# Modulation rows of parts two to five moved beside the output projections, and read as whole rows

## The chip, the cores and the metric

The kernel runs on one core of one Trainium2 chip. The metric is the device time of one execution in microseconds, the median of several runs. Engines are named as in the profile: PE is TensorE (PEld its weight loads), DVE is VectorE, ACT is ScalarE, POOL is GpSimd, SP is SyncE, which issues most transfers.

## The reference, cut to what matters

One decoder layer on a sequence of 512 tokens of width 1024, all in float32. Six modulation vectors of 1024 values each come from the condition vector, and are needed at very different times:

```
mod = (silu(c) @ w_ada + b_ada)          # w_ada is 1024 x 6144
sh1, sc1, g1, sh2, sc2, g2 = split(mod, 6)
h = rms(x) * (1 + sc1) + sh1
x = x + g1 * mixer(h)                    # SSD, attention and pooling, then w_out
h = rms(x) * (1 + sc2) + sh2
x = x + g2 * (relu(h @ w_ff1)**2 @ w_ff2)
```

Parts zero and one (sh1, sc1) are needed at once. Part two (g1) is needed after w_out, parts three and four (sh2, sc2) in the second norm, part five (g2) in the second feed-forward product. The mixer projects h by w_in to the inputs of three branches and three gates, and adds

```
sigmoid(gate_ssd) * (y_ssd @ w_ssd_out) + sigmoid(gate_attn) * (y_attn @ w_attn_out) + sigmoid(gate_pool) * (y_pool @ w_pool_out)
```

## The kernel before

Activations lie transposed, 128 channels by 512 tokens a block. Every float32 operand of a large product is split into a high and a low part (h and l in the names); a product is three matmuls, low by high, high by high and high by low (`mm3`, L293 to L296). Weights come in pairs of 128 rows: `wstream` (L283) loads a pair (`raw`, four buffers, 0.5 MB, L287), ACT rounds it to the high part `wh` (L279), DVE subtracts to the low part `wl` (L280); `wh` and `wl` have three buffers each. One pair feeds 24 matmuls in `gemm_feat` (L298) or `gemm_tok` (L310). After each pair `wstream` calls `tick` (L263).

`tick` is where other work is traced between the matmuls. It runs one piece of the list `side`, which holds the steps of attention, SSD and pooling, and on every second call one piece of the list `background`. That list has 32 pieces, `ada_later(part, k)` for parts two to five and eight values of k. One piece makes 128 values of one modulation vector, with `ada_load` (L237) and `ada_dot` (L243): 128 rows of the transposed w_ada, 1024 values each, are loaded as two halves of 128x512 into two blocks; each half is multiplied on DVE with `crow`, the silu of the condition copied to all partitions, and summed along the row (L246); the two sums are added (L248) and the bias added (L256) into a column of `modv`.

The order of the products after the first two (Q0 and K0, ordered by hand in a manual schedule up to about 60 us) is, in the names used below: Q1, K1, Q2, K2, V0, V1, V2 (attention inputs), BCC, XS0, Z0, XS1, Z1 (SSD inputs), gate GA0, attention projection, GA1, attention projection, U0, U1 (pool inputs), gate GS0, SSD projection, GS1, SSD projection, GP0, pool projection, GP1, pool projection, then w_out and the feed-forward part. Each has four pairs of weights and so four ticks, the two attention projections two. Before the change the 32 pieces therefore fall on the 64 ticks of Q1 to U0.

The SSD heads (`ssd_heads`, L904) broadcast rows of a small table `prow` to all partitions with a transfer each (`M`, L912), DVE and ACT make decay factors from it (L917 to L926), and PE uses them (L932); `ssd_states` makes the tiles X (L882) and prev (L895) from which PE makes the states. `project` (L747) multiplies a branch's product with its gate `sg` on DVE (L751).

Blocks of 128x512 come from a ring of 49 places (`blk`, `free`): the place that was given back first is taken first, and a new tile in a place waits until all users of the old one are done. Beside it there are four places of twice that size with the names L0, L1, N0 and N1 (pool `exp`): they hold the tokens in another order for Q1 to V2, then the attention output `oh`, `ol` until the second attention projection, and from w_out on two pairs of the first feed-forward weights (L1130), later sums of weights.

Outside the manual schedules a planner orders each engine's instructions by their place in the trace, with `high_priority` stretches moved ahead and with work that is ready taken forward into idle time, and it sets the semaphores. Each engine then runs its list in order. So does SP: a transfer that waits for its place holds all transfers behind it on SP's queue.

Of the kernel before, what the change touches and what calls it, by code (L numbers as in the profile page):

```python
# [10 lines left out]
F32 = mybir.dt.float32  # L11
F32R = mybir.dt.float32r
AF = mybir.ActivationFunctionType
ALU = mybir.AluOpType
# [3 lines left out]
P = 128  # L18
D = 1024
T = 512  # L20
# [78 lines left out]
def kernel(ctx: ExitStack, tc: tile.TileContext, a: dict, out: bass.AP, dbg=None):  # L99
    nc = tc.nc  # L100
# [5 lines left out]
    exp = ctx.enter_context(tc.tile_pool(name="exp", bufs=1))  # L106
# [6 lines left out]
    def uid(s):  # L113
        cnt[0] += 1
        return f"{s}_{cnt[0]}"

    class Slots:
# [12 lines left out]
        def free(self, t):  # L130
            self.idle.append(self.used.pop(id(t))[0])
# [3 lines left out]
    def blk(name, dt=F32):  # L135
        return sb.take(name, dt)
# [12 lines left out]
    def small(shape, name, bufs=1, dt=F32):  # L149
        return sm.tile(shape, dt, tag=name, name=uid(name), bufs=bufs)  # L150
# [7 lines left out]
    def show(name, ap):  # L158
        if dbg is not None:
            dbg(name, ap)  # L160

    mm = nc.tensor.matmul
    V, S = nc.vector, nc.scalar
# [20 lines left out]
    crow2 = small([P, 2, T], "crow")  # L184
    crow = [crow2[:, i, :] for i in range(2)]
# [3 lines left out]
    def vc(name, i=0, n=1):  # L189
        return vec[:, VCOLS[name][0] + i : VCOLS[name][0] + i + n]  # L190
# [43 lines left out]
        return sums  # L234


    def ada_load(part, k):  # L237
        wa = [blk("wa") for _ in range(2)]
        for i in range(2):
            nc.sync.dma_start(wa[i], a["w_ada"][part * 8 + k][:, i * T : (i + 1) * T])  # L240
        return wa

    def ada_dot(wa, o):  # L243
        d = small([P, 2], "dot", 4)
        for i in range(2):
            V.scalar_tensor_tensor(wa[i], wa[i], 1.0, crow[i], ALU.mult, ALU.mult, accum_out=d[:, i : i + 1])  # L246
        free(*wa)
        V.tensor_tensor(o, d[:, 0:1], d[:, 1:2], ALU.add)  # L248

    modv = small([P, 4, 8], "modv")  # L250

    def ada_later(part, k):
        def go():
            o = modv[:, part - 2, k : k + 1]
            ada_dot(ada_load(part, k), o)
            V.tensor_tensor(o, o, vc("b_ada", part * 8 + k), ALU.add)  # L256
        return go


    background = [ada_later(part, k) for part in (2, 3, 4, 5) for k in range(8)]  # L260
    side, ticks = [], [0]

    def tick(n=1):  # L263
        ticks[0] += 1
        for _ in range(n):
            if side:
                side.pop(0)()
        if ticks[0] % 2 == 0 and background:
            background.pop(0)()

    def flush():
        while side:
            side.pop(0)()
# [9 lines left out]
    def wstream(w, nk, ch, k0=0, ahead=None):  # L283
        for kp in range(nk // 2):
            with tc.high_priority(offset=AHEAD if ahead is None else ahead):
                raw = raws.tile([P, 2, T], F32, tag="raw", name=uid("raw"))
                nc.sync.dma_start(raw, w[ch, k0 // 2 + kp])  # L287
                wh, wl = wsplit(raw, [P, 2, T])
            for i in range(2):
                yield 2 * kp + i, wh[:, i, :], wl[:, i, :]  # L290
            tick()
# [6 lines left out]
    def gemm_feat(w, nk, ch, ah, al, k0=0):  # L298

        ps = [acc() for _ in range(4)]  # L300
        for k, wh, wl in wstream(w, nk, ch, k0):
            for j in range(4):
                cs = slice(j * P, (j + 1) * P)
                mm3(ps[j], wh[:, cs], wl[:, cs], ah[k], al[k], k == 0, k == nk - 1)
        return ps
# [13 lines left out]
    def split(x, name):  # L319
        h, l = blk(name + "h", F32R), blk(name + "l", F32R)  # L320
        S.copy(h, x)
        V.tensor_tensor(l, x, h.bitcast(F32), ALU.subtract)
        return h, l
# [17 lines left out]
    with tc.manual_schedule(engines={E.DVE, E.Activation, E.PE, E.SP}):  # L341
# [14 lines left out]
        def ada_whole(part, k):  # L356
            pool, tag = homes["rrrhlhlrrrhlhlhl"[2 * k + 1 - part]]
            w = pool.tile([P, 2, T], F32, tag=tag, name=uid("wada"))
            src = a["w_ada"][part * 8 + k].rearrange("p (i t) -> p i t", i=2)
            if k:  # L360
                nc.sync.dma_start(w, src)
            else:
                for i in range(2):
                    nc.sync.dma_start(w[:, i, :], src[:, i, :])
            return w
# [5 lines left out]
        wa = [ada_whole(1, 0), ada_whole(0, 0)]  # L371
# [77 lines left out]
        var, rt, r, t = (small([P, 4], "rx" + n) for n in "vryt")  # L449
# [59 lines left out]
        for k in range(8):  # L509
# [8 lines left out]
            if k < 7:  # L518
                wa = [ada_whole(1, k + 1), ada_whole(0, k + 1)]
                w_load(k + 1)  # L520
                d = small([P, 2], "dot", 4)
# [221 lines left out]
    def gate(c, ch):  # L743
        ps = gemm_feat(w_in, 8, c + ch, hh, hl)
        return evac(ps, "sg", AF.Sigmoid)

    def project(w, nk, ch, yh, yl, sg, first=False, last=False):  # L747
        ps = gemm_feat(w, nk, ch, yh, yl)
        with tc.high_priority(offset=SOON):
            for j in range(4):  # L750
                V.tensor_tensor(sg[j], ps[j], sg[j], ALU.mult)  # L751
        free(*ps)
        for j in range(4):
            if first:
                mixed.append(sg[j])
                continue
            m = mixed[4 * ch + j]
            V.tensor_tensor(m, m, sg[j], ALU.add)
            free(sg[j])
            if last:  # L760
                x, y = split(m, "mx")
                free(m)
                mh.append(x)
                ml.append(y)
        if ch == 1:
            free(*yh, *yl)


    v3 = lambda t: t.rearrange("p (c h) -> p c h", h=16)
    st = {}  # L770

    def ssd_steps():

# [329 lines left out]
    for ch in range(2):  # L1103
        sg = gate(GS, ch)
        flush()
        project(a["w_ssd_out"], 8, ch, yh, yl, sg)
    show("yn", [h.bitcast(F32) for h in yh + yl])
    show("pool", [h.bitcast(F32) for h in ph_ + pl_])
    for ch in range(2):
# [374 lines left out]
```

## Time and profile before

| | before |
|---|---|
| median of 3 runs | 1096.73 us (1096.44 to 1097.73) |
| the profiled execution | 1098.25 us |
| its span, first to last instruction | 1096.5 us |
| granted TensorE clock | 1.000 |
| PE busy | 1087.1 us, 99% of the span |
| DVE busy | 717.4 us, 65% |
| ACT busy | 527.8 us, 48% |
| products with `crow` of parts two to five | 64, 43.1 us, mean 688 ns |
| idle time of DVE before them | 20.0 us |
| half rows loaded | 64 of 256 KB, median 3.6 us to landing |

A row of a group has the line, the engine, the operation, what it writes and reads, the shapes and the count, then busy time, the mean of one, and the idle time of the engine just before with what ended it. A row in order of time has the start, the duration and the count; in square brackets stands the idle time before it and what ended that. A row of a line or tile has the shortest, median and longest duration in ns and the first and last start in us. A row of waits says who waited for whom, the sum in us, how often, and the longest.

### The profile page before, as it was taken

What the parts mean: (1) busy time and instruction counts of PE and PEld (TensorE: products, weight loads), DVE (VectorE), ACT (ScalarE), POOL (GpSimd) and SP (SyncE); (2) the same over time, 40 slices, a digit from 0 to 9 for tenths busy, and PEclk for the clock granted to TensorE, in tenths of its full rate; (3) what the DMA queues carried; (4) which work ended last, traced back from release to release, by engine and by line L of the source; (5) the groups of instructions that cost most, each with busy time, mean ns of one, the idle gap of its engine ahead of it and who ended that gap; (6) DMA issues with size and microseconds to landing.
All of it is one profiled execution on the core that took longest, in us unless ns stands there. A gap on an engine that the chain in (4) does not pass through costs nothing.

```text
span 1096.5 us, 14976 instructions
## 1 busy us (share of the span) xinstructions
PE 1087.1 (99%) x5806; PEld 927.0 (85%) x5806; DVE 717.4 (65%) x1383; ACT 527.8 (48%) x845; POOL 3.6 (0%) x10
## 2 busy tenths in 40 slices
PE   9999999999999999999999999999999999999998
PEld 7878888888887877888888888899889989989987
DVE  8975874582776778568843424577787587686664
ACT  8965875543695536625432123354344334335330
POOL 0000000000000000000000000000000000000000
PEclk9999999999999999999999999999999999999999
DMA  9853342443542354321232325360214224134032
GB/s 349 306 183 98 128 134 86 152 168 102 173 125 87 117 181 136 104 97 58 96 115 97 106 96 163 97 230 1 79 57 154 65 90 136 59 114 135 20 116 77
DMA packets 46666, 133.98 MB, mean 122 GB/s; under 512 B 5362, under 2 KB 6130, under 8 KB 46596
## 3 DMA queue, kind: packets, MB, share of 16 engines
q1 hardware_dynamic: 45392, 130.28, 36.0%
q0 software_dynamic: 480, 1.57, 0.5%
q10 hardware_dynamic: 724, 1.18, 0.3%
q8 instruction: 45, 0.74, 0.3%
q14 instruction: 25, 0.20, 0.1%
HBM read 130.89 MB, written 2.13 MB: 121 GB/s over the span
## 4 chain that ended last, share of the span: by engine, by line
PE 87%; ACT 4%; DVE 3%; DMA 3%; issue 1%; SPq 0%; ACTq 0%; DVEq 0%
PE psacc L294 22%; PE psacc L296 22%; PE psacc L295 22%; PE psacc L1345 11%; PE psacc L534 4%; DMA M<-prow 2%; PE psS L613 1%; DMA wa<-in_w_ada_dram 1%; DVE conv L850 1%; ACT wh L279 1%; PE pso L729 1%; PE pso L727 1%; DVE wl L280 1%; PE pskT L597 0%; PE psqT L592 0%
## 5 line engine op out<-in xcount | busy, mean ns | idle before, releaser
L280 DVE TENSOR_TENSOR wl<-raw,wh 128x1024 fp32r<-128x1024 f32 x140 | 171.0, 1222 | 192.2 <-ACT wh L279 190.9
L279 ACT CAST wh<-raw 128x1024 fp32r<-128x1024 f32 x140 | 146.8, 1050 | 241.1 <-PE psacc L295 168.8
L294 PE MATMUL psacc<-hl,wh 128*128 128x512 f32 x416 | 166.6, 401 | 3.4 <-DVE X L882 2.2
L295 PE MATMUL psacc<-hh,wh 128*128 128x512 f32 x416 | 162.1, 390 | 0.0
L296 PE MATMUL psacc<-hh,wl 128*128 128x512 f32 x416 | 162.0, 390 | 0.0
L295 PE MATMUL psacc<-ah,wh 128*128 128x512 f32 (+1 forms) x260 | 100.4, 386 | 0.0
L294 PE MATMUL psacc<-al,wh 128*128 128x512 f32 (+1 forms) x260 | 100.4, 386 | 0.0
L296 PE MATMUL psacc<-ah,wl 128*128 128x512 f32 (+1 forms) x260 | 100.3, 386 | 0.0
L294 PEld LDWEIGHTS psacc<-hl,wh 128*128 128x128 f32 x416 | 78.2, 188 | 21.7 <-DVE X L882 2.7
L295 PEld LDWEIGHTS psacc<-hh,wh 128*128 128x128 f32 x416 | 78.2, 188 | 16.9 <-issue 1.4
L296 PEld LDWEIGHTS psacc<-hh,wl 128*128 128x128 f32 x416 | 78.1, 188 | 16.7
L294 PE MATMUL psacc<-wl,rh 128*128 128x512 f32 x192 | 76.9, 401 | 0.0
L296 PE MATMUL psacc<-wh,rl 128*128 128x512 f32 x192 | 75.5, 393 | 0.0
L295 PE MATMUL psacc<-wh,rh 128*128 128x512 f32 x192 | 75.3, 392 | 0.0
L296 PEld LDWEIGHTS psacc<-ah,wl 128*128 128x128 f32 x260 | 48.8, 188 | 9.9
L294 PEld LDWEIGHTS psacc<-al,wh 128*128 128x128 f32 x260 | 48.9, 188 | 9.7
L295 PEld LDWEIGHTS psacc<-ah,wh 128*128 128x128 f32 x260 | 48.9, 188 | 9.6
L1405 DVE SCALAR_TENSOR_TENSOR xr<-psacc,modv,xr 128x512 f32<-128x512 f32 (+1 forms) x65 | 44.7, 739 | 18.6 <-PE psacc L296 18.6
L246 DVE SCALAR_TENSOR_TENSOR wa<-wa,crow 128x512 f32<-128x512 f32 x64 | 43.1, 688 | 20.0 <-DMA wa<-in_w_ada_dram 20.0
L296 PEld LDWEIGHTS psacc<-wh,rl 128*128 128x128 f32 x192 | 36.0, 188 | 7.6
L294 PEld LDWEIGHTS psacc<-wl,rh 128*128 128x128 f32 x192 | 36.1, 188 | 7.3 <-ACT qT L593 0.2
L295 PEld LDWEIGHTS psacc<-wh,rh 128*128 128x128 f32 x192 | 36.1, 188 | 7.0
(408 smaller groups left out, 2360.8 us busy)
## 6 DMA issues: line engine op xcount, KB each, us to landing
raw<-in_w_in_dram SPq DMA_DIRECT2D x80, 512.0 KB, 3.5
raw<-in_w_ff_dram SPq DMA_DIRECT2D x52, 512.0 KB, 3.7
wa<-in_w_ada_dram SPq DMA_DIRECT2D x64, 256.0 KB, 3.6
wada<-in_w_ada_dram SPq DMA_DIRECT2D x14, 512.0 KB, 7.8
rawl<-in_w_ff_dram SPq DMA_DIRECT2D x12, 512.0 KB, 3.5
wst<-in_w_in_dram SPq DMA_DIRECT2D x16, 256.0 KB, 7.8
M<-prow SPq DMA_DIRECT2D x16, 256.0 KB, 3.8
raw<-in_w_ssd_out_dram SPq DMA_DIRECT2D x8, 512.0 KB, 3.5
```

What stands on the lines that cost most here:

```text
L246: V.scalar_tensor_tensor(wa[i], wa[i], 1.0, crow[i], ALU.mult, ALU.mult, accum_out=d[:, i : i + 1])
L279: S.copy(wh, raw)
L280: V.tensor_tensor(wl, raw, wh.bitcast(F32), ALU.subtract)
L294: mm(ps, lhsT=wh, rhs=xl, start=first, stop=False)
L295: mm(ps, lhsT=wh, rhs=xh, start=False, stop=False)
L296: mm(ps, lhsT=wl, rhs=xh, start=False, stop=last)
L534: mm(ps[j], lhsT=t[:, j, :], rhs=w, start=first, stop=last)
L613: mm(so[b], lhsT=qT[:, b * P : (b + 1) * P], rhs=kT[:, (b + 1) * P - n : (b + 1) * P], start=True, stop=True)
L727: mm(od, lhsT=vs[kb][:, hs], rhs=pT[b // 2][:, cs : cs + P], start=(b == 0), stop=False, skip_group_check=True)
L729: mm(ov[:, b, :], lhsT=vs[b][:, hs], rhs=pT[0][:, b * P : (b + 1) * P], start=False, stop=(gi == 2 and b == 3), skip_group_check=True)
L1345: mm(o, lhsT=x[:, cs], rhs=y, start=first and k == 0 and j == 0 and n == 0, stop=k == 3 and n == 2, skip_group_check=True)
L1405: V.scalar_tensor_tensor(xT[d][:, ts], p[:, : ts.stop - ts.start], modv[:, 3, d : d + 1], xT[d][:, ts], ALU.mult, ALU.add)
```

## The change

Three things change together. A piece of `background` loads one whole row of 128x1024 with one transfer of 0.5 MB into one of the four wide places (L0, L1, N0, N1 in turn), multiplies and sums it with one DVE instruction straight into `modv`, and adds the bias; the halves, their two blocks of the ring and the add of two sums are gone. `tick` runs as many pieces as `st["pace"]` says: none up to and in the first SSD gate GS0, two in each of the two SSD projections, one in the products behind the first of them (GS1, GP0, the first pool projection and GP1). With four ticks each these are 8, 4, 8, 4, 4 and 4 pieces. And the dictionary `st` is made earlier in the text, since `tick` reads it.

```
-    def ada_load(part, k):
-        wa = [blk("wa") for _ in range(2)]
-        for i in range(2):
-            nc.sync.dma_start(wa[i], a["w_ada"][part * 8 + k][:, i * T : (i + 1) * T])
-        return wa
-
-    def ada_dot(wa, o):
-        d = small([P, 2], "dot", 4)
-        for i in range(2):
-            V.scalar_tensor_tensor(wa[i], wa[i], 1.0, crow[i], ALU.mult, ALU.mult, accum_out=d[:, i : i + 1])
-        free(*wa)
-        V.tensor_tensor(o, d[:, 0:1], d[:, 1:2], ALU.add)
-
     modv = small([P, 4, 8], "modv")
 
     def ada_later(part, k):
         def go():
             o = modv[:, part - 2, k : k + 1]
-            ada_dot(ada_load(part, k), o)
+            w = exp.tile([P, 2, T], F32, tag=("L0", "L1", "N0", "N1")[k % 4], name=uid("wada"))
+            nc.sync.dma_start(w, a["w_ada"][part * 8 + k].rearrange("p (i t) -> p i t", i=2))
+            V.scalar_tensor_tensor(w, w, 1.0, crow2, ALU.mult, ALU.mult, accum_out=o)
             V.tensor_tensor(o, o, vc("b_ada", part * 8 + k), ALU.add)
         return go
...
-    side, ticks = [], [0]
-
-    def tick(n=1):
-        ticks[0] += 1
-        for _ in range(n):
-            if side:
-                side.pop(0)()
-        if ticks[0] % 2 == 0 and background:
-            background.pop(0)()
+    side, st = [], {}
+
+    def tick():
+        if side:
+            side.pop(0)()
+        for f in background[: st.get("pace", 0)]:
+            f()
+        del background[: st.get("pace", 0)]
...
     for ch in range(2):
         sg = gate(GS, ch)
         flush()
+        st["pace"] = 2
         project(a["w_ssd_out"], 8, ch, yh, yl, sg)
+        st["pace"] = 1
```

More of the change, by code (lines that the diff above doesn't have):

```diff
@@ L769 @@
     v3 = lambda t: t.rearrange("p (c h) -> p c h", h=16)
-    st = {}
     def ssd_steps():
```

## Prediction

> **What bounds the kernel now.** I read the page first, then the stretches, then what TensorE (PE) waited for, then the order of time around its two dearest waits.
>
> ```profile
> span 1096.5 us, 14976 instructions
> PE 1087.1 (99%) x5806; PEld 927.0 (85%) x5806; DVE 717.4 (65%) x1383; ACT 527.8 (48%) x845; POOL 3.6 (0%) x10
> ```
>
> PE is busy for 1087.1 of 1096.5 us. Only 9.4 us of idle time are left, and a change that takes no matmul away can win only what PE waits. By stretch (us, then PE, PEld, DVE, ACT and POOL busy, clock, DMA share, GB/s):
>
> ```profile
> 0.00:50.00 50.00, 47.63 (x233) 39.46 (x234) 44.80 (x93) 44.25 (x65) 0.20 (x4) 1.00 0.97 358
> ...
> 250.00:500.00 250.00, 246.47 (x1282) 202.19 (x1281) 163.09 (x310) 138.28 (x205) 0.00 (x0) 1.00 0.38 122
> 500.00:704.00 204.00, 204.00 (x908) 168.93 (x907) 96.32 (x149) 65.67 (x85) 0.00 (x0) 1.00 0.33 107
> ```
>
> PE idles 3.5 us between 250 and 500, in the SSD and attention part, and not at all between 500 and 704, where the branch projections run. VectorE (DVE) is 65% busy in the first of these (163.09 of 250) and 47% in the second (96.32 of 204). From 250 to 500 it also does 28 half modulation rows, and stands 12.1 us for their loads (busy, mean ns, then idle time before them):
>
> ```profile
> L246 DVE SCALAR_TENSOR_TENSOR wa<-wa,crow 128x512 f32<-128x512 f32 x28 | 19.1, 688 | 12.1 <-DMA wa<-in_w_ada_dram 12.1
> ```
>
> What ended PE's waits from 60 to 500 us (total, times, longest):
>
> ```profile
> PE psacc L294 <- DVE X L882: 2.2, 1, 2.2
> PE psacc L294 <- DVE conv L935: 0.5, 1, 0.5
> PE psacc L294 <- ACT prev L895: 0.5, 1, 0.5
> PE psacc L294 <- ACT pT L711: 0.2, 1, 0.2
> ```
>
> These are 3.4 of the 3.5 us. What one costs is read from matmul starts, since ends are modelled:
>
> ```profile
> 428.16 0.39 PE L295 MATMUL psacc<-hh,wh 128*128 128x512 f32 x1
> 428.39 0.40 PE L296 MATMUL psacc<-hh,wl 128*128 128x512 f32 x1
> 431.01 0.50 PE L294 MATMUL psacc<-hl,wh 128*128 128x512 f32 x1 [2.22 <-DVE X L882]
> 431.35 0.40 PE L295 MATMUL psacc<-hh,wh 128*128 128x512 f32 x1
> ```
> ```profile
> 387.99 0.40 PE L296 MATMUL psacc<-hh,wl 128*128 128x512 f32 x1
> 388.90 0.50 PE L294 MATMUL psacc<-hl,wh 128*128 128x512 f32 x1 [0.51 <-DVE conv L935]
> 389.23 0.40 PE L295 MATMUL psacc<-hh,wh 128*128 128x512 f32 x1
> ```
>
> Undisturbed, a matmul starts 0.23 us after the last (428.16 to 428.39). The first wait costs 2.62 - 0.23 = 2.39 before the late start and 0.34 - 0.23 = 0.11 after it: 2.50 us. The second costs 0.68 + 0.10 = 0.78. So a wait costs its idle time and 0.28 more; the 0.5 of prev is 0.78 and the 0.2 of pT 0.48. All four together are 4.5 us, **the most that can be won here**.
>
> [...]
>
> Both larger waits lead back to the modulation rows that are to be moved. On DVE in order of time:
>
> ```profile
> 385.43 0.69 DVE L246 SCALAR_TENSOR_TENSOR wa<-wa,crow 128x512 f32<-128x512 f32 x1 [1.22 <-DMA wa<-in_w_ada_dram]
> ...
> 386.96 1.23 DVE L280 TENSOR_TENSOR wl<-raw,wh 128x1024 fp32r<-128x1024 f32 x1
> 388.10 0.74 DVE L935 SCALAR_TENSOR_TENSOR conv<-conv,dcol,psy 128x512 f32<-128x512 f32 x1
> ...
> 427.29 0.68 DVE L924 TENSOR_SCALAR M<-M,pc 128x128 f32<-128x128 f32 x3 [2.92 <-DMA M<-prow]
> 427.88 2.48 DVE L751 TENSOR_TENSOR sg<-psacc,sg 128x512 f32<-128x512 f32 x4
> 430.27 0.68 DVE L882 TENSOR_TENSOR X<-psX,dt 128x512 f32<-128x512 f32 x1
> ```
>
> At 385 DVE stands 1.22 us for a row of w_ada, multiplies it, and the split of the weights and L935, for which PE waits, come behind: without the row L935 is done 2.7 us sooner (1.22, and 386.96 - 385.43 = 1.53). At 427 DVE stands 2.92 us for a broadcast of prow, and X comes behind that and the four products with sg. The chain of waits leads there from a load of w_ada (start, us):
>
> ```profile
> 396.30 4.94 DMA wa<-in_w_ada_dram
> ...
> 402.66 4.31 DMA M<-prow
> ```
>
> and on SyncE's queue the broadcasts (L912) wait for places which w_ada held before:
>
> ```profile
> SPq L912 <- DVE wa L246: 8.1, 4, 3.9
> ```
>
> **The change, part by part.** It removes 64 half-row loads, 64 products with sum and 32 adds of two halves, and moves the rest from the stages Q1 to U0 to ssd_out (two rows a tick), the second SSD gate and the two pool gates and first pool projection (one a tick): 8 + 4 + 8 + 4 + 4 + 4 = 32. Old costs:
>
> ```profile
> L240 SPq DMA_DIRECT2D wa<-in_w_ada_dram x64: 327/328/2078, 42.4 to 475.9; - x64
> L246 DVE SCALAR_TENSOR_TENSOR wa<-wa,crow x64: 679/688/696, 53.9 to 480.6; 128x512 f32<-128x512 f32 x64
> L246 DVE DVE_READ_ACCUMULATOR wa<-wa,crow x64: 78/83/93, 54.6 to 481.2; 128x1 f32 x64
> ```
> ```profile
> L248 DVE TENSOR_TENSOR modv<-dot x32: 149/157/161, 58.4 to 481.4; 128x1 f32<-128x1 f32 x32
> L256 DVE TENSOR_TENSOR modv<-modv,vec x32: 147/156/163, 58.6 to 483.7; 128x1 f32<-128x1 f32 x32
> ...
> L1116 DVE SCALAR_TENSOR_TENSOR A<-modv,vec x1: 168/168/168, 333.5 to 333.5; 128x8 f32<-128x8 f32 x1
> ```
> ```profile
> DVE wa L246 <- DMA wa<-in_w_ada_dram: 20.0, 14, 4.1
> ```
>
> From DVE before 484 us go 64 x (0.688 + 0.083) + 32 x (0.157 + 0.156) = 59.4 us of work and 20.0 us of standing for loads; SyncE's queue loses 64 issues of 0.33 and their waits ahead of weights and broadcasts. DVE has idle time there in any case, so these 79 us are worth what they held up on PE: 2.50 + 0.78 = 3.28. The other two waits were ended by ACT, and I leave them.
>
> New costs have a model in the whole rows of parts 0 and 1 at the start:
>
> ```profile
> L388 DVE SCALAR_TENSOR_TENSOR wada<-wada,crow x7: 1219/1220/1222, 19.8 to 49.8; 128x1024 f32<-128x1024 f32 x7
> ...
> DMA to landing us min/median/max: 4.4/7.8/9.0
> ```
>
> A row costs DVE 1.22 + 0.08 (reading the sum, as above) + 0.16 (bias) = 1.46 us, 46.7 us in all, and SyncE 32 issues of 0.33 us. Two rows a tick meet these stretches (first and third gemm of the SSD projection's four):
>
> ```profile
> 551.00:573.00 22.00, 22.00 (x98) 18.21 (x98) 8.71 (x11) 5.26 (x6) 0.00 (x0) 1.00 0.39 129
> ...
> 595.00:617.00 22.00, 22.00 (x98) 18.20 (x97) 6.74 (x7) 4.99 (x7) 0.00 (x0) 1.00 0.30 97
> ```
>
> Eight rows add 11.7 us: 20.4 and 18.4 busy of 22, cost nothing on PE. The cover is the split weights: three pairs of buffers hold 24 matmuls each, 5.5 us; a pair is refilled when PE has left it, so two pairs, 11.0 us, stand between DVE and PE, less cast and split, 2.5 us if the cast is no longer than the 1.23 of the split: 8.5 us. DVE has time to spare there now (waits from 551 to 704):
>
> ```profile
> DVE wl L280 <- ACT wh L279: 92.4, 24, 4.2
> ```
>
> If that cover is gone, each us that DVE is late is a us on PE. A row that has not landed holds the split behind it on DVE, and PE waits for the split; on SyncE a row whose place is not free holds the next weight load. Landing is bounded by
>
> ```profile
> raw<-in_w_ssd_out_dram SPq DMA_DIRECT2D x8, 512.0 KB, 3.5
> ```
>
> and the 7.8 us of the rows at the start, where DMA ran at 358 GB/s. Two rows and one weight load of 0.52 MB in 5.5 us ask 286 GB/s, nearer the full start, so I take 6 us. A place then turns round in 1.46 + 0.33 + 6 = 7.8 us, at 7.8 us landing in 9.6, both under the 11.0 us in which four places are asked for once.
>
> The results are read late enough: A2 (L1116), which ran at 333.5, moves behind part four, but its readers stand in the second norm after w_out; the residual of part two likewise:
>
> ```profile
> L1143 DVE SCALAR_TENSOR_TENSOR xr<-psacc,modv,xr x4: 744/744/747, 724.5 to 726.4; 128x512 f32<-128x512 f32 x4
> ```
>
> A2's early run also shows that the planner moves ready work forward, so rows may run before their ticks, in DVE's gaps.
>
> What no row shows is the new order that the planner makes of everything from 60 us on, with other blocks (64 fewer turns of the ring of 49). Bounds: all four waits gone, -4.5 us; none gone and one as dear as the dearest seen in addition, +2.5. I take the two named waits as gone and one new wait of the smallest size, 0.48: **3.28 - 0.48 = 2.8 us**. The profiled execution took 1098.25 us, 1.75 around its span; it becomes 1095.45. The median of the runs, 1096.73, lies 1.52 below it: **1093.9 us**.
>
> **The rivals.**
> *The wait at 431 stays.* What DVE stood for there is a broadcast, not a row; DMA, cast and the four products with sg are still ahead of X. For it: 2.48 us of sg lie ahead of X whatever lands. Against it: X need be only 2.22 us sooner, and the queue's 8.1 us go. Only 0.78 is won: 1096.0.
> *All four go,* because ACT's chain hangs on the same broadcasts: 1096.73 - 4.5 = 1092.2. Against it: ACT's own work is the same.
> *Slower: DVE's queue in the two projections of ssd_out.* Its idle time there falls to 1.6 and 3.6 us. With the cover of 8.5 a row may be late by (1.6 + 8.5) / 8 = 1.3 us on average before PE stands; from there each us counts eight times. Shown is 20.0 / 64 = 0.31 on average, at most 4.1. Halfway, 2.2, PE would lose 17.6 - 10.1 = 7.5 and 17.6 - 12.1 = 5.5: 1093.9 + 13 = 1106.9. Against it: the average shown, and that planned work runs ahead of its ticks.
> [...]
> *The new order has a new wait* of 2.50 and keeps the old ones: 1099.2.
>
> **How the numbers follow.** Forecast 0.44 (own range 1092.9 to 1094.8), the wait stays 0.32, all gone 0.12, DVE's queue 0.07, new wait 0.05. Within 0.2% (about what a measurement of this kernel can tell) is 1094.5 to 1098.9. Faster: 0.12 and 0.42 of the forecast's 0.44, 0.54. Same: the other 0.02 and 0.32, 0.34. Slower: 0.07 and 0.05, 0.12. The range goes from 1092.0, under the bound of all four, to 1098.8, and leaves out the 0.12 above.
>
> **What would show it.** Right: no wait of PE for X or L935 over 0.3 us between 250 and 500; DVE busy there down by some 26 us from 163.09 (28 x 0.771 + 14 x 0.313); 32 products of 128x1024 at 1.22 us; PE still without idle time from 500 to 704. Wrong: PE waits for wl or a product with sg between 500 and 704 (the slow rival), or X still ends a wait near 431 with DVE standing for M ahead of it (the first rival).

## The result, and the profile after

The changed kernel takes 1097.96 us (1096.75 to 1100.75) against 1096.04 us (1095.24 to 1097.73) of the kernel before beside it, a ratio of 1.0021 (95% interval 1.0012 to 1.0029): **slower by 0.2%**, where 1093.9 was forecast. The profiled execution took 1100.18 us; it is one of four of the 13 whose mean granted clock is 0.998, and one of the longest. Its page begins:

```profile
span 1098.4 us, 14808 instructions
PE 1087.7 (99%) x5806; PEld 928.4 (85%) x5806; DVE 709.0 (65%) x1287; ACT 520.2 (47%) x839; POOL 3.6 (0%) x10
```

Everything that was to be removed is removed (DVE has 96 instructions fewer), and the same 5806 matmuls take 1.9 us longer from first to last. By stretch (us, then PE, PEld, DVE, ACT and POOL busy, clock, DMA share, GB/s), the changed kernel:

```profile
250.00:500.00 250.00, 246.90 (x1279) 203.02 (x1279) 152.77 (x252) 129.64 (x199) 0.00 (x0) 0.99 0.40 128
500.00:704.00 204.00, 203.60 (x906) 168.45 (x905) 121.07 (x216) 67.37 (x87) 0.00 (x0) 1.00 0.44 146
465.00:500.00 35.00, 34.06 (x205) 27.25 (x204) 32.63 (x67) 9.21 (x13) 0.00 (x0) 1.00 0.83 285
500.00:551.00 51.00, 50.60 (x231) 41.72 (x230) 50.30 (x116) 26.17 (x39) 0.00 (x0) 1.00 0.39 128
551.00:704.00 153.00, 153.00 (x677) 126.73 (x676) 70.77 (x101) 41.20 (x49) 0.00 (x0) 1.00 0.45 152
```

and the kernel before in two of these:

```profile
465.00:500.00 35.00, 35.00 (x210) 28.35 (x209) 24.51 (x46) 11.00 (x15) 0.00 (x0) 1.00 0.27 94
500.00:551.00 51.00, 51.00 (x233) 42.24 (x232) 40.79 (x87) 26.29 (x40) 0.00 (x0) 1.00 0.25 83
```

In the projections, from 551 on, PE never stands, as forecast. From 465 to 551, in the inputs of the pooled branch and the gate GS0, PE now stands where it did not, and DVE is full there: 32.63 of 35 us and 50.30 of 51, against 24.51 and 40.79. And in 250 to 500 the mean clock is 0.99. What ended PE's five longest waits in the changed kernel (total, times, longest):

```profile
PE pssx L400 <- DVE sq L409: 2.3, 1, 2.3
PE psacc L282 <- ACT prev L882: 2.0, 1, 2.0
PE pswarm L393 <- DVE ones L362: 1.1, 1, 1.1
PE psacc L282 <- DVE conv L922: 0.9, 1, 0.9
PE psmix L284 <- DVE wl L268: 0.4, 1, 0.4
```

The first and third belong to the start-up. X, pT and the old wait for conv are gone. The wait for prev, 0.5 us before, is 2.0 us long, and two new ones stand behind it. Since the order of the products is the same, the start of the first matmul of a product, taken from the order of time of each trace, shows where the difference arises (in us, the differences taken before rounding):

| start of | before | after | difference |
|---|---|---|---|
| Q1 (end of the start-up) | 60.36 | 61.05 | +0.69 |
| XS1 | 333.69 | 334.46 | +0.77 |
| Z1 | 359.32 | 363.20 | +3.88 |
| first attention projection | 413.06 | 415.77 | +2.71 |
| second attention projection | 454.81 | 454.98 | +0.16 |
| U1 | 495.06 | 495.22 | +0.16 |
| first SSD projection | 551.72 | 553.62 | +1.90 |
| w_out | 704.04 | 705.94 | +1.90 |

So 3.7 us are won between Z1 and the second attention projection (+3.88 to +0.16; every version below without the rows there takes the same 91.8 us for this stretch, the kernel before 95.5), 3.1 are lost in XS1, another 1.7 in U1 and GS0, and 0.7 in the start-up, whose instructions the change does not touch (in the profiles of the experiments below Q1 starts from 0.15 us before to 0.91 after that of the kernel before, so these 0.7 are put down to no part of the change).

**The loss in XS1.** PE of the changed kernel in order of time:

```profile
336.70 0.39 PE L284 MATMUL psacc<-hh,wl 128*128 128x512 f32 x1
339.11 0.79 PE L282 MATMUL psacc<-hl,wh 128*128 128x512 f32 x1 [2.02 <-ACT prev L882]
339.70 0.63 PE L283 MATMUL psacc<-hh,wh 128*128 128x512 f32 x1
340.12 0.63 PE L284 MATMUL psacc<-hh,wl 128*128 128x512 f32 x1
...
342.61 0.40 PE L284 MATMUL psacc<-hh,wl 128*128 128x512 f32 x1
342.85 0.40 PE L282 MATMUL psacc<-hl,wh 128*128 128x512 f32 x1
```

The matmul that waits starts a new sum in psacc; it waits until ACT has copied prev out of psst. The wait costs 339.11 - 336.70 - 0.23 = 2.18 us. Then the matmuls start 0.42 to 0.43 us apart instead of 0.23 until 342.3; the nine steps from 339.11 to 342.85 cost 3.74 - 9 x 0.23 = 1.67 more. The granted clock is the cause that the trace gives: over 339.0 to 342.5 it is

```profile
339.00:342.50 3.50, 3.39 (x8) 2.72 (x9) 1.06 (x2) 0.56 (x2) 0.00 (x0) 0.51 0.47 150
```

Together 3.85 us, less the 0.78 that prev cost in the same place before: 3.07, against 3.11 in the table. Why prev is late stands on ACT, in order of time, first the changed kernel:

```profile
334.35 0.40 ACT L909 ACTIVATE M<-M,npc 128x128 f32<-128x128 f32 x1 [3.32 <-DMA M<-prow]
334.77 1.28 ACT L321 ACT_TABLE_LOAD   x1
336.06 0.60 ACT L321 ACTIVATE z<-psacc 128x512 f32<-128x512 f32 x1
336.56 1.04 ACT L267 CAST wh<-raw 128x1024 fp32r<-128x1024 f32 x1
337.49 1.09 ACT L321 ACTIVATE z<-psacc 128x512 f32<-128x512 f32 x2
338.46 0.60 ACT L882 COPY prev<-psst 128x512 f32<-128x512 f32 x1
```

and the kernel before:

```profile
335.19 1.09 ACT L333 ACTIVATE z<-psacc 128x512 f32<-128x512 f32 x2
336.15 0.60 ACT L895 COPY prev<-psst 128x512 f32<-128x512 f32 x1
336.62 0.63 ACT L333 ACTIVATE z<-psacc 128x512 f32<-128x512 f32 x1
337.44 0.40 ACT L922 ACTIVATE M<-M,npc 128x128 f32<-128x128 f32 x1 [0.19 <-DMA M<-prow]
```

Before, prev came first and a decay factor M behind it. Now an M, one of the second group of SSD heads, stands ahead of the z, of a weight cast and of prev, and waits 3.32 us for its broadcast of `prow`. In the kernel before, the M behind prev was the last of the first group, whose eight broadcasts were issued from 243 to 334 us; now those eight are out by 295, and the next M in line is one of the second group. Its broadcast, the ninth, is issued at 330.85, after SP has waited for its place:

```profile
SPq L899 <- DVE M L913: 5.3, 1, 5.3
...
330.85 0.33 SPq L899 DMA_DIRECT2D M<-prow  x1
```

**The loss in U1 and GS0.** The rows run long before their ticks (tile of the wide places; shortest, median, longest in ns, first and last start in us):

```profile
L243 SPq DMA_DIRECT2D wada<-in_w_ada_dram x32: 327/328/495, 460.2 to 573.9; - x32
L244 DVE SCALAR_TENSOR_TENSOR wada<-wada,crow x32: 1217/1220/1228, 463.8 to 584.2; 128x1024 f32<-128x1024 f32 x32
```

The wide places are given back by the second attention projection, which runs from 455 to 466; the planner takes rows forward to there, over 85 us before the first tick that asks for one. Of the 32 products 20 start before 551. Of DVE's order of time ahead of the wait for conv (nothing is idle between these):

```profile
489.86 1.22 DVE L268 TENSOR_TENSOR wl<-raw,wh 128x1024 fp32r<-128x1024 f32 x1
...
492.79 1.23 DVE L244 SCALAR_TENSOR_TENSOR wada<-wada,crow 128x1024 f32<-128x1024 f32 x1
...
496.40 1.23 DVE L268 TENSOR_TENSOR wl<-raw,wh 128x1024 fp32r<-128x1024 f32 x1
497.54 0.70 DVE L232 TENSOR_TENSOR sums<-sums,sq 128x512 f32<-128x512 f32 x1
498.14 0.75 DVE L922 SCALAR_TENSOR_TENSOR conv<-conv,dcol,psy 128x512 f32<-128x512 f32 x1
```

PE at the end of it:

```profile
497.62 0.39 PE L283 MATMUL psacc<-hh,wh 128*128 128x512 f32 x1
498.94 0.51 PE L282 MATMUL psacc<-hl,wh 128*128 128x512 f32 x1 [0.94 <-DVE conv L922]
```

That costs 1.32 - 0.23 = 1.09 and 0.11 in the late start; the 0.40 for wl near 535 costs 0.68 by the prediction's rule (0.28 more than its idle time). Together 1.88, against 1.74 in the table.

### The profile page after: what moved, and what is told of

It reads as the page before. It is cut to its first block, busy times and chain, and to the rows that moved or that the text cites. A ratio compares the mean times of both kernels' runs of the same rounds, so it can differ in the third digit from the quotient of the medians.

```text
span 1098.4 us, 14808 instructions
## 1 busy us (share of the span) xinstructions
PE 1087.7 (99%) x5806; PEld 928.4 (85%) x5806; DVE 709.0 (65%) x1287; ACT 520.2 (47%) x839; POOL 3.6 (0%) x10
## 4 chain that ended last, share of the span: by engine, by line
PE 89%; DVE 5%; ACT 3%; DMA 2%; issue 1%; SPq 0%; DVEq 0%; ACTq 0%
PE psacc L282 22%; PE psacc L284 22%; PE psacc L283 22%; PE psacc L1334 11%; PE psacc L522 4%; PE psS L601 1%; DMA wada<-in_w_ada_dram 1%; DVE conv L837 1%; DMA M<-prow 1%; DVE win L964 1%; DVE wl L268 1%; PE pspT L698 1%; PE pskT L585 0%; PE pso L717 0%; PE psqT L580 0%
## 5 line engine op out<-in xcount | busy, mean ns | idle before, releaser
L284 PEld LDWEIGHTS psacc<-hh,wl 128*128 128x128 f32 x416 | 78.5, 189 | 16.9
L244 DVE SCALAR_TENSOR_TENSOR wada<-wada,crow 128x1024 f32<-128x1024 f32 x32 | 38.8, 1221 | 6.0 <-DMA wada<-in_w_ada_dram 6.0
```

Source lines behind the costliest of these rows:

```text
L244: V.scalar_tensor_tensor(w, w, 1.0, crow2, ALU.mult, ALU.mult, accum_out=o)
L284: mm(ps, lhsT=wl, rhs=xh, start=False, stop=last)
```

## The experiments

The theory: two losses, one by the order on ACT near 337 us, one by rows that DVE takes forward into the pooled branch. The rivals to be told apart: that the rows themselves bring both; that prev would be late on any queue; and that it is the whole rows, not their place, that lose the time. PE's waits are told without those of the start-up.

### No rows at all

Both the load and the product of a row are left out; these modulation values are then the bias alone.

```
-            w = exp.tile([P, 2, T], F32, tag=("L0", "L1", "N0", "N1")[k % 4], name=uid("wada"))
-            nc.sync.dma_start(w, a["w_ada"][part * 8 + k].rearrange("p (i t) -> p i t", i=2))
-            V.scalar_tensor_tensor(w, w, 1.0, crow2, ALU.mult, ALU.mult, accum_out=o)
-            V.tensor_tensor(o, o, vc("b_ada", part * 8 + k), ALU.add)
+            V.tensor_copy(o, vc("b_ada", part * 8 + k))
```

> Leaves out the rows of parts two to five altogether (no load, no product: these modulation values are the bias alone, so the output is another), with everything else as in the changed kernel. Theory (two separate losses: the planner's new order on ACT around 336 us, which comes from the rows being absent there, and the rows themselves, run early between 460 and 550): PE's wait for prev near 337 stays at about 2 us, the waits near 497 and 534 go, the time is the changed kernel's less 1.7, about 1096.3. Rival (the rows' own work and traffic cost everything): all three waits go, about 1092.

Measured: 1097.23 us against 1096.29, ratio 1.001 (0.9999 to 1.002). PE's only wait:

```profile
PE psacc L279 <- ACT prev L879: 1.8, 1, 1.8
```

A kernel with no row to compute is no faster than the one before. On ACT the M stands ahead of prev as in the changed kernel and waits 3.24 us for its broadcast. So the wait does not come from where the rows went, but from their absence here: without them the planner makes this order. The waits at 498 and 535 are gone with the rows. The time is 0.9 above the 1096.3 expected; 6 of these 12 executions have a mean clock of 0.998, the profiled one has not.

### The rows held behind the pooled branch

The products of the rows may start only behind the last split of the pooled branch; their loads are not held.

```
         for f in background[: st.get("pace", 0)]:
-            f()
+            with tc.issue_after(st["edge"].ins):
+                f()
...
-        V.tensor_tensor(l, x, h.bitcast(F32), ALU.subtract)
+        st["low"] = V.tensor_tensor(l, x, h.bitcast(F32), ALU.subtract)
...
             x, y = split(cur, "pd")
+            st["edge"] = st["low"]
```

> The changed kernel, with the products of the rows held on DVE behind the last split of the pooled branch, near 543 us; the loads are not held. Theory: the waits near 497 (0.9) and 534 (0.4) go, the wait for prev near 337 stays, about 1096.3 against 1098.0. Rival (DVE's queue in the output projections, the slow rival of the prediction): 32 rows now fall between 543 and 720, PE waits for wl or for a product with a gate there, 1098 or more.

Measured: 1095.98 us against 1096.29, ratio 1.0003 (0.9993 to 1.0013). The waits at 498 and 535 are gone, prev's stays:

```profile
PE psacc L283 <- ACT prev L883: 1.9, 1, 1.9
```

In its profile nothing is lost from the second attention projection on (0.44 and 0.47 us ahead of the kernel before at both ends). No row runs before 539.5 now (463.8 in the changed kernel). The second loss is the rows taken forward. The M still stands ahead of prev on ACT, and waits 3.19 us.

### prev copied by DVE, alone and with the rows held

```
-                        S.copy(pv, sp)
+                        V.tensor_copy(pv, sp)
```

> The changed kernel, with the first prev of each group copied by DVE instead of ACT, so that it no longer stands behind the broadcast of prow on ACT's queue. Theory: the 2.0 us wait near 337 shrinks to under 0.6, with it the granted clock stays 1.00 in all executions; about 1096.3 against 1098.0. Rival (the late broadcast reaches PE by another way, the weights' high part or the copies of z behind it on ACT): a wait of 1 to 2 us stays near 337 to 350 and the time is 1097.5 or more.

> The changed kernel with both edits. Theory: both losses go, the 3.7 us won in the two attention gates stay, about 1094.5, faster than the kernel before by 1.5. Rival (a new order brings new waits each time): 1096 to 1098, with a wait over 0.5 us at a place that none of the other kernels has.

Measured: alone 1099.84 us, ratio 1.0034 (1.0022 to 1.0045); with the rows held 1097.9, ratio 1.0012 (1.0001 to 1.0024). Both expectations failed: the wait for prev stays in both, 2.1 and 2.3 us. The reason, on DVE of the first of the two in order of time:

```profile
337.18 1.23 DVE L268 TENSOR_TENSOR wl<-raw,wh 128x1024 fp32r<-128x1024 f32 x1 [2.38 <-ACT wh L267]
338.32 0.69 DVE L882 COPY prev<-psst 128x512 f32<-128x512 f32 x1
```

prev has left ACT's queue, but on DVE it stands behind a weight split that waits 2.38 us for its cast, and the cast stands on ACT behind the same M (which waited 3.00 us in this profile). This edit did not take the cause away and so tells nothing against it; it is the M that has to move.

### The order on ACT alone

For the second group of SSD heads, the instructions that make M (on ACT and DVE) may start only behind the first prev. No transfer is touched; the lines under the `with` are indented and otherwise as they were.

```
-                        S.copy(pv, sp)
+                        st["prev", g] = S.copy(pv, sp)
...
+            with tc.issue_after(st["prev", 0].ins) if g else ExitStack():
                 S.activation(e[fs, P:], M[fs, P:], AF.Exp, scale=-1.0)
...
                 S.activation(M, M, AF.Exp, scale=-1.0)
```

> The changed kernel, with one instruction moved: the planner had taken a decay factor of the second SSD group (the operation on M at 334.4 us on ACT, which stands 3.3 us for its broadcast) ahead of the copies of z and the first prev of the first group; it is held behind that prev on ACT. No transfer moves. Theory (that instruction's place in ACT's queue is the whole cause of the wait near 337): the wait goes from 2.0 to under 0.3 us, no half clock, the waits near 497 and 534 stay: 1098.0 less 2.2 and the mean of the half clock, 0.4, about 1095.4. Rival (ACT is late there anyway, as in the kernel before, where prev was waited for by 0.5): a wait of 0.5 or more stays, 1096.5.

Measured: 1095.91 us against 1096.29, ratio 1.0001 (0.9992 to 1.001). On ACT prev is back ahead of M:

```profile
334.77 0.59 ACT L882 COPY prev<-psst 128x512 f32<-128x512 f32 x1
335.23 0.62 ACT L321 ACTIVATE z<-psacc 128x512 f32<-128x512 f32 x1
335.72 0.42 ACT L910 ACTIVATE M<-M,npc 128x128 f32<-128x128 f32 x1
```

and PE waits only for the other two:

```profile
PE psacc L282 <- DVE conv L923: 0.9, 1, 0.9
PE psmix L284 <- DVE wl L268: 0.4, 1, 0.4
```

The first loss is the M ahead of prev. No execution of this kernel has a mean clock under 0.999. At the second attention projection its profile is 4.43 us ahead of the kernel before, at the first SSD projection 2.77: the second loss, 1.66, stands alone.

The time from the first matmul of XS1 to that of Z1 gives the size of the first loss in each profile, with and without the half clock:

| versions | XS1 to Z1, us |
|---|---|
| order on ACT held (this one and the four below that hold it) | 24.83 |
| kernel before | 25.63 |
| M ahead of prev, clock full throughout (no rows; halves, below) | 26.95; 26.81 |
| M ahead of prev, with the half clock (changed; rows held; prev on DVE, alone and held) | 28.74; 28.61; 28.79; 29.01 |

Of what lies over the 24.83, the prediction's rule for a wait (its idle time and 0.28 more) leaves 0.02 to 0.04 us in the three profiles without the half clock and 1.6 in each of the four profiles with it. So the half clock costs 1.6 us. Without it the wait of 2.02 in the changed kernel would have cost some 1.5 more than prev's 0.78 before, by that rule.

### Both

> The changed kernel with both holds: the rows' products on DVE behind the pooled branch's last split, and the second group's decay factor on ACT behind the first prev. Theory: all of PE's waits between 60 and 704 us over 0.3 us are gone, and the 3.7 us won in the attention gates stay: about 1093.6, 2.5 under the kernel before. Rival (new waits appear wherever the old ones go): 1096, with a wait over 0.5 us at a new place.

Measured: 1094.26 us against 1096.29, ratio 0.9986 (0.9977 to 0.9995), and again, beside other kernels:

> Whole rows with both holds a second time, beside the two others on their chip, to compare the three. Theory: 1094.3 within 0.5, faster than the kernel before by about 2.

1094.02 us against 1095.97, ratio 0.9983 (0.9974 to 0.9992). Behind the start-up PE waits for nothing that the profile names: the rival, that new waits appear where the old ones go, did not come true. The first time is 0.7 above the 1093.6 expected. The stretches of the first of the two runs:

```profile
250.00:500.00 250.00, 249.86 (x1302) 206.20 (x1301) 146.19 (x232) 132.56 (x203) 0.00 (x0) 1.00 0.30 103
500.00:704.00 204.00, 204.00 (x909) 168.89 (x908) 136.20 (x245) 66.54 (x86) 0.00 (x0) 1.00 0.51 180
```

Against the changed kernel the medians fall by 2.05 us with the order on ACT, 1.98 with the rows held and 3.70 with both. These runs were not beside each other; taken each against the kernel before beside it, the steps are 2.30, 2.23 and 3.95. Either way the two losses add up within 0.6 us, and each step is known to about 1 us. **This version is faster than both kernels**, than the one before by 0.14% with an interval of 0.05 to 0.23%.

### The halves kept, at the new pace

One part of the change undone: two half rows in blocks of the ring, as before, but at the new ticks.

```
+    def ada_load(part, k):
...
+    def ada_dot(wa, o):
...
-            w = exp.tile([P, 2, T], F32, tag=("L0", "L1", "N0", "N1")[k % 4], name=uid("wada"))
-            nc.sync.dma_start(w, a["w_ada"][part * 8 + k].rearrange("p (i t) -> p i t", i=2))
-            V.scalar_tensor_tensor(w, w, 1.0, crow2, ALU.mult, ALU.mult, accum_out=o)
+            ada_dot(ada_load(part, k), o)
```

> Undoes one part: the rows are loaded and multiplied as halves in two blocks of the ring, as before, at the new pace; the wide places are unused. Theory (the place in the order costs, not the shape): the wait for prev near 337 stays, and since blocks are free earlier than the wide places, rows are still taken forward into the pooled branch; each costs DVE 0.3 us more; 1098.0 to 1098.6. Rival (the wide places, which come free at 465 us, are what draws the rows into the pooled branch): the waits near 497 and 534 go, 1096.3.

Measured: 1096.07 us against 1096.29, ratio 1.0004 (0.9995 to 1.0012). My own expectation of where the halves would run fell, the rival's held:

```profile
L246 DVE SCALAR_TENSOR_TENSOR wa<-wa,crow x64: 677/684/694, 552.5 to 636.3; 128x512 f32<-128x512 f32 x64
```

No half row runs before 552. That blocks of the ring are not free in the pooled branch is the likely reason; the profile shows only that two of the loads waited 1.4 and 0.3 us for that branch's products to give blocks back. prev's wait stays at 1.7 us, behind the same M (3.15 us), and the other two waits are gone. So moving the rows away brings the first loss, and the wide places, which happen to come free between 460 and 466, bring the second. With the order on ACT mended as well:

> Halves in blocks of the ring at the new pace, with the second group's decay factor held on ACT behind the first prev. Theory (what pays is the move out of the attention and SSD stage; whole rows in the wide places add nothing that PE sees): the same as with whole rows and both holds, 1094.3, within 0.5. Rival (the 64 loads and 32 adds more cost PE time beside the projections): 1095 or more, with waits of PE between 546 and 640.

Measured: 1094.24 us against 1095.97, ratio 0.9983 (0.9974 to 0.9992). As good as whole rows held back: whole or half makes no difference that these runs can tell.

### Four rows a tick

The version with both mends, at twice the pace in the SSD projections (`st["pace"] = 4`), meant to press the slow rival.

> Whole rows with both holds, at four rows a tick in the two projections of ssd_out in place of two. It tries the prediction's slow rival: 16 rows and the 8.7 us already there are 32.1 us of DVE work in the 22 us of the first projection, over the 22 + 8.5 that the split weights cover. If DVE did them where they stand, PE would wait 1.6 us or more for wl there, 1096 or more. Theory (the planner puts the splits ahead of the rows and lets the rows run on into the gate behind): no such wait, 1094.3 within 0.5.

Measured: 1094.43 us against 1095.97, ratio 0.9985 (0.9976 to 0.9994). In the fullest stretch, and for the rows:

```profile
550.00:572.00 22.00, 22.00 (x99) 18.22 (x98) 18.68 (x39) 4.22 (x4) 0.00 (x0) 1.00 0.92 333
L244 DVE SCALAR_TENSOR_TENSOR wada<-wada,crow x32: 1212/1218/1227, 535.9 to 608.6; 128x1024 f32<-128x1024 f32 x32
```

DMA moves 333 GB/s, DVE is busy for 18.68 of 22 us and stands for rows six times in the whole profile, 8.5 us in all; PE never stands. But the edit did not do what it was meant to. At two rows a tick the products run from 536.3 to 607.1, and 10 of them start in this stretch; at four they run from 535.9 to 608.6, and again 10 of them start there, not the 16 asked for. That the four wide places and the landings set this rate is likely and was not tested. So 32.1 us of DVE work never stood in 22 us, and this run says no more of the cover than the two before it.

## Why the prediction was wrong

**What came of the range and the signs.** The forecast was a gain and the result is a loss; that 1097.96 lies inside 1092.0 to 1098.8 is luck, since no way that the prediction names leads there: those inside its range end at 1096.0 or below. Of the signs named, the wait for X is gone, 32 products of 1.22 us are there; but a wait for conv of 0.94 us, over the 0.3 allowed, stands at 499, and PE waits 0.40 us for wl at 535, where it was to have no idle time.

**The two waits, 3.28.** Right. They are gone, and pT's 0.48 with them, 3.76 in all; the table has 3.7 (1.17 + 2.54). At X, DVE of the changed kernel does not stand for M any more:

```profile
426.47 0.48 DVE L911 TENSOR_SCALAR M<-M,pc 128x128 f32<-128x128 f32 x2
426.94 2.74 DVE L739 TENSOR_TENSOR sg<-psacc,sg 128x512 f32<-128x512 f32 x4
429.60 0.68 DVE L869 TENSOR_TENSOR X<-psX,dt 128x512 f32<-128x512 f32 x1
```

The first rival, that this wait stays, is refuted.

**"One new wait of the smallest size, 0.48".** This is the step that failed. The new order cost 3.07 in XS1, with prev's old 0.78 already taken off, and 1.74 to 1.88 in U1 and GS0: ten times the term, and nearly twice the upper bound of 2.5, which allowed one wait as dear as the dearest seen and left out both a second one and a half clock behind it. Without the half clock, which 9 of the 13 executions do not show in their mean clock, it is some 1.5 and 1.74 to 1.88, together 3.3 (an estimate): still seven times the term. With the start-up: -3.76 + 3.07 + 1.88 + 0.69 = 1.88, against +1.90 measured at w_out. The new order was the one term that no row showed, and I gave it the smallest price rather than a middle one. "I leave them" of the waits ended by ACT was the same mistake: the one for prev was already 0.5 us long and had a queue ahead of it that the change reshuffles.

**"Rows may run before their ticks, in DVE's gaps".** Seen and not priced. They ran in the pooled branch and GS0, where DVE had 10.5 us to spare of 35 and then 10.2 of 51; 2.4 and 0.7 are left. The working priced DVE only from 551 on. That the wide places come free with the second attention projection was known; the stretch between that and the first tick was the one to look at.

**The rows' own price.** Right: 1.22 for a product and 0.08 for its sum; the median landing is 4.6 us in the changed kernel and 5.4 to 6.2 where the rows are held back, taken as 6. DVE's busy time from 250 to 500 was to fall by 26 us and fell by 10.3, since rows came back into its end; with both mends it falls by 16.9. The other 9 are no work that the change adds. The 26 was a sum of durations, and DVE's records overlap (above, one that starts at 496.40 and lasts 1.23 is followed at 497.54), which busy time counts once. By durations the rows take 25.9 us away and DVE falls by 22.3: the kernel with both mends is 3.7 us ahead at 500, which brings 3.6 us of later work into the stretch. The remaining 5.4 is overlap.

**The cover in the projections.** Nothing contradicts it: PE is busy for all of 153 us from 551 to 704 in the changed kernel, and in the versions with the rows held, where 25 or 26 of the 32 products fall behind 551, it has no wait there either. The slow rival did not come true, but the state that it needs, rows late by over 1.3 us on average, was never reached: in the three of these with both mends DVE stood 5.7 to 8.5 us for all 32, 0.27 each at most on average.

**The rival "a new wait and the old ones kept", 1099.2.** Half right: a new wait came, of about that size, but the old ones went. It had a chance of 0.05.

**From profile to median.** With all four waits gone the prediction gives 1092.2; the versions that have none left take 1094.0 to 1094.4. Their profiled spans, 1091.9 to 1092.8, are 3.7 to 4.6 below that of the kernel before, about the bound of 4.5; their medians are 1.5 to 2.0 below. The profiled execution of the kernel before, 1098.25, lies some 2 us above its median in all these comparisons, and above the 1.52 that the prediction took off. So the waits read from it may be dearer than those of its usual execution; only one execution has a trace, so this stays open. The forecast also started from a median of three runs, 1096.73; with 13 to 34 runs it is 1095.97 to 1096.29.

Open also is why the planner puts that M ahead once the rows are gone. That it does so with no rows at all, with rows held, and with halves is shown; that the first group's broadcasts go out earlier once no rows stand among them (by 295 us, not 334) is seen, and would let the second group's M come up at this point, but no run tests it.

## What to carry to other kernels

Where a planner orders in-order queues, taking work out of a stretch changes the order of what stays: compare each engine's order before and after around the waits that are nearly late, and look for an operation of a later stage that now stands, waiting for a transfer, ahead of an urgent one. Work that is moved runs where its buffers come free, not where it is traced, so price it in every stretch from that point on, or hold it there explicitly. A change whose gain is a few waits of PE deserves a middle price for the new order, not the smallest.

## What the runs showed of the hardware that was not expected

**The half clock.** An idle time of 2.02 us was followed by 3.4 us at half the granted clock, which made the 2.18 us of the wait 3.85: in the profile of the changed kernel the clock is 0.50 from 339.10 to 342.52, and 1.00 from 4.6 to there and from there to 1096. The kernel before idles 2.22 us at 429 in its profile, and no half clock follows (1.00 from 425 to 436). The profiles in which PE waits over 1.5 us at one place between 60 and 1000, with the mean granted clock of the profiled execution:

| profile | idle time of PE | mean clock | half clock behind it |
|---|---|---|---|
| kernel before | 2.22 at 429 | 1.000 | none |
| no rows | 1.80 | 1.000 | none |
| halves | 1.67 | 1.000 | none |
| rows held | 1.89 | 0.998 | yes |
| changed | 2.02 | 0.998 | yes |
| prev on DVE and rows held | 2.28 | 0.998 | yes |
| prev on DVE | 2.07 | 0.998 | yes |

The other five profiles have no wait of PE over 0.94 us there, and a mean clock of 0.999 or 1.000. The 2.28 us that the changed kernel waits in its start-up are not followed by a half clock either (1.00 from 6 to 16). So the length of a wait alone does not tell these apart: 1.89 us had a half clock behind it and 2.22 had none. What decides is not shown. In each of the four profiles with the half clock the wait cost 1.6 us more than by the prediction's rule, which was read in part from the wait of 2.22; with no rows and with halves it cost 0.04 us more at most. The other executions have only a mean clock. It is 0.998 or less in 30 of 71 executions of the six versions with M ahead of prev, in 3 of 55 of the five with the order on ACT held, and in 9 of 88 of the kernel before. What idles in those few of the 55 no profile shows.
